# Turning keys and queries in 32x32 blocks on VectorE and by short store runs, in place of TensorE turns

## The chip, the cores and the metric

The kernel runs on one core of a Trainium2 chip. The metric is the device time of one execution in microseconds. Before the change it is 1336.66 us, the median of 3 runs (1335.41 to 1338.84).

The engines are named as in the profile: PE is TensorE's matmul queue and PEld its weight loads, DVE is VectorE, ACT is ScalarE, POOL is GpSimd, SP is SyncE, which only issues DMAs here. ACT and POOL issue DMAs too.

## The reference

One layer of a diffusion block over 512 tokens of width 2048, with 256 context tokens, all in float32. Cut to what matters:

```python
h  = rmsnorm(x) modulated by the conditioning vector      # 512 x 2048
hc = rmsnorm(ctx) modulated likewise                      # 256 x 2048
p  = h @ w_in                                             # q, k, v, z_a, u_b, z_b, g_a, g_b
kc, vc = rmsnorm per head of (hc @ w_in[:, K]), hc @ w_in[:, V]
q = rope(rmsnorm per head of q) * 128 ** -0.5             # 12 heads of 128
k = rope(rmsnorm per head of k)                           # 4 heads of 128
attn = softmax(q @ [k, kc].T) @ [v, vc]                   # 3 query heads per key head, 768 keys
y_a = (attn * silu(z_a)) @ w_proj_a
y_b = (fft2(u_b) * silu(z_b)) @ w_proj_b
x  = x + gate * ((sigmoid(g_a) * y_a + sigmoid(g_b) * y_b) @ w_out)
return rmsnorm(x) * final_g
```

The score product needs queries and keys with the head's 128 channels along the partitions. The projections leave them with the tokens along the partitions, so both must be turned somewhere between the projection and the scores.

## The kernel before

Matrix products are made in float32 accuracy from float32r halves: each operand is split into a high part (ACT, a copy, L162) and a low part (DVE, a subtraction, L163), and `mm3` issues three matmuls (L294 high by high, L295 high by low, L296 low by high). `split_from` is the helper for one split.

The projection after the first stage is made in groups of 1024 output columns, g = 0 to 7, of the kinds `KINDS`: three "qz" groups (queries of four heads and their z), two "gate", one "kv" (g = 5), two "gate". Each group computes its four quarters (two token halves by two column halves) from seven products (P1, Q5, P2, Q6, P7, Q3, Q4) of four weight pieces each. A piece of 512 KB is loaded by SP's queue (L198, L201) or added onto a running sum by an accumulating POOL DMA (L250), combined by DVE where needed (L239, L241), split by ACT and DVE, and then used by 12 matmuls. `get` splits pieces ahead of their use, up to as many as there are buffers for split pieces (3, or 5 for most of the time). A stop of ACT, DVE or the loads therefore reaches TensorE only once these ready pieces are used up.

After P2 the quarter (half 0, queries) is ready, after Q4 the quarter (half 1, queries); after P7 and Q3 those of z. `qz_done` and, for g = 5, `kv_done` take them:

- `rotated` (L827) squares each head on ACT for its norm (L836), multiplies by cosines and sines on DVE (L838, L840), adds the two (L843) and scales by the norm's root (L844). The result r lies in the buffer qr, the only one for this, and so the next rotated half can't begin to write before the stores of the one before have landed.
- Two stores per half, issued by ACT (L858 for queries and z, L868 for keys and values), write 128 tokens each to a DRAM buffer, one 512-byte run per token and head. `qz_d` has for each head and token partition the queries and z of its four token tiles.
- In the kv group the context's keys and values are made beside the tokens' (`Context`). `keys` normalizes the context keys in half of a buffer called cxe, which shares its place with a raw load buffer, and stores them (L926).

After the last query half, `context_norm` (L942) writes a diagonal into the first columns of qr, for the context's norms. After group 5, the space of qr is given to two more raw load buffers; loads into them on SP's queue wait for the key stores to land.

The program is written in the order of the loops, with a list `jobs` of deferred steps of which one is run per weight piece. A planner then sets the order on each engine's queue by its own costs and due times, so that steps of `rotated` lie scattered among the splits.

Attention runs 48 steps, one per head and tile of 128 queries. `scores` multiplies with all 768 keys into a pair of PSUM banks tagged "x", takes the maximum on DVE (L1117) and the exponentials on ACT (L1119); `turn` turns the probabilities on TensorE (L1135), `values` multiplies them by the values, and `filler` fills in products of the other branch. Around the change:

- `load_head` loads queries and z of a head from qz_d by a POOL DMA (L1003).
- `turn_queries` (L1014) turns a head's four query tiles on TensorE into a PSUM bank (L1016) that the products with the values also use, and splits them from there. This is done at the second step of the head before.
- `get_keys` (L1005) takes the raw keys of a key head from their load buffer, turns six tiles of 128 keys on TensorE into an "x" pair (L1009), and splits them from PSUM. The first key head is taken before the last product of the last group, the others at steps 10, 22 and 34.

Of the kernel before, what the change touches and what calls it, by code (L numbers as in the profile page):

```python
# [18 lines left out]
P = 128  # L19
# [88 lines left out]
def block_kernel(ctx, tc, xT, ctx_rows, ctx_toks, x, c_row, w_ss, w_gate, vecs, qkg, rope, dft_c, dft_s,  # L108
# [718 lines left out]
    def rotated(half, v, t2):  # L827

        v = v.rearrange("p t (h d) -> p t h d", h=4)
        r, t2 = new_q(), t2.rearrange("p t (h d) -> p t h d", h=4)  # L830
        ss = sums[:, 8 * half : 8 * half + 8]
        r5 = lambda w: w.rearrange("p h (a f j) -> p h a f j", a=2, f=2)
        for b in range(2):
            cosb, sinb = (turning[:, i, 2 * half + b, None, :].broadcast_to([P, 4, HD]) for i in range(2))
            for h in range(4):
                nc.scalar.activation(t2[:, b, h, :], v[:, b, h, :], ACT.Square,  # L836
                                     accum_out=ss[:, 4 * b + h : 4 * b + h + 1])
            nc.vector.tensor_tensor(r[:, b], v[:, b], cosb, op=ALU.mult)  # L838
# [5 lines left out]
        nc.vector.tensor_tensor(r, r, ss.rearrange("p (t h) -> p t h", t=2)[:, :, :, None].broadcast_to([P, 2, 4, HD]),  # L844
                                op=ALU.mult)
        return r

    def qz_done(half, c, v, t):

        if c:  # L850
            e = pair("x" if half else "y")
            nc.scalar.activation(e, v, ACT.Tanh, scale=0.5)
            nc.vector.scalar_tensor_tensor(v, e, 1.0, v, op0=ALU.add, op1=ALU.mult)
            r = v.rearrange("p t (h d) -> p t h d", h=4)
        else:
            r = rotated(half, v, pair("y"))
        for b in range(2):
            nc.scalar.dma_start(qz_d[4 * group.g : 4 * group.g + 4, :, c, 2 * half + b, :].rearrange("h p d -> p h d"),  # L858
                                r[:, b])

    by_group = lambda v: v.rearrange("g p d -> p g d")

    def kv_done(half, c, v, t):


        r = v.rearrange("p t (g d) -> p t g d", g=4) if c else rotated(half, v, pair("y", 1) if half else pair("x"))
        for b in range(2):
            nc.scalar.dma_start(by_group((v_d if c else k_d)[:, :, 2 * half + b, :]), r[:, b])  # L868

    class Context:  # L870

# [45 lines left out]
        def keys(self, b, v):  # L917
# [8 lines left out]
            nc.scalar.dma_start(by_group(k_d[:, :, 4 + b, :]), k4)  # L926


    cparts = qr[:, :1792].rearrange("p (f j c) -> p f j c", f=7, j=2)
# [69 lines left out]
    qz, qs, kv = {}, {}, {}  # L999

    def load_head(h):
        qz[h] = take((2, 4, HD))
        nc.gpsimd.dma_start(qz[h], qz_d[h])  # L1003

    def get_keys(g):  # L1005
        raw = get(("K", g))
        tk = flat(pair("x"))
        for t in range(KT):
            nc.tensor.transpose(tk[:, t * P : (t + 1) * P], raw[:, t * P : (t + 1) * P], ident)  # L1009
        keys = tiles(g)  # L1010
        split_from(tk[:, :NKEY], *(w[:, :NKEY] for w in keys))
        kv[g] = tuple(keys) + get(("V", g))

    def turn_queries(h, tq):  # L1014
        for t in range(4):
            nc.tensor.transpose(tq[:, t * P : (t + 1) * P], qz[h][:, 0, t, :], ident)  # L1016
        qs[h] = take((2, T), F32R)
        split_from(tq, qs[h][:, 0, :], qs[h][:, 1, :])

    load_rotations(qkg[:, 0:2, :])  # L1020
    for g, kind in enumerate(KINDS):
# [13 lines left out]
        for name in ONE_GROUP:  # L1035
# [20 lines left out]
            elif (g, name) == (LAST, "Q4"):  # L1056
                hl_pools[:] = [p for p in hl_pools if not isinstance(p, int)]
                get_keys(0)
                jobs.append(lambda: turn_queries(0, pair("y")[:, 0, :]))
            group.run(name)  # L1060
    gvs.close()
    evs.close()
# [60 lines left out]
    def divide(i):  # L1123

        h, t = divmod(i, 4)
        z = qz[h][:, 1, t, :]
# [15 lines left out]
    def values(half):  # L1142
# [4 lines left out]
        for k in range(KT):  # L1147
            mm3(av[:, :256], vh[:, k, :], vl[:, k, :], pth[:, k, :], ptl[:, k, :], k == 0, k == KT - 1)
        for t in range(2):
            nc.tensor.transpose(av[:, 256 + t * P : 256 + (t + 1) * P], qz[h][:, 1, 2 * second + t, :], ident)  # L1150
        if second:
            give(qz.pop(h))
            if h % GQ == GQ - 1:
# [25 lines left out]
    for i in range(NSTEP + 3):  # L1179
# [18 lines left out]
            turn(i - 1)  # L1198
            divide(i - 1)
        if t == 1 and h + 1 < NH:  # L1200
            turn_queries(h + 1, b1())
        if want > filled:
            fill(want - filled)
            filled = want
# [360 lines left out]
```

## Time and profile before

| what | value |
|---|---|
| median of 3 runs | 1336.66 us |
| span of the profiled execution | 1334.5 us |
| PE busy | 1299.7 us, 97% |
| DVE busy | 978.1 us, 73% |
| ACT busy | 653.8 us, 49% |
| POOL busy | 138.0 us, 10% |
| DMA, mean rate | 218 GB/s, 291.28 MB |
| q1 (loads and stores issued by SP) | 37.2% of 16 engines |
| q0 (issued by POOL) | 28.7% |
| q10 (issued by ACT) | 5.1%, 22464 packets, 22.81 MB |
| TensorE's granted clock, mean | 0.998 |

The execution's own time outside the span is not shown, so the span is set beside the median of the runs. The three qz groups lie from about 170 to 400 us, with their last steps to 420, the kv group from about 557 to 671, attention from about 815 to 1005. Busy time of PE is pipelined: a 512-column matmul is shown with 0.39 us but the next one starts 0.23 us later, so starts tell more than durations. A number in brackets behind a row of the timeline is the engine's idle time just before it, with what ended it. A wait is given with its total, its count and its longest. In a row of a DMA queue stand packets, MB and the share of the time of 16 engines; in a row of DMA issues the KB of each and the median time from issue to landing in us.

### The profile page before, as it was taken

To read this page: it belongs to the slowest core of one execution; us is meant where nothing else is said; L and a number is where in the kernel's file an instruction comes from. 1 tells how busy PE (TensorE), PEld (TensorE's weight loads), DVE (VectorE), ACT (ScalarE), POOL (GpSimd) and SP (SyncE) were. 2 spreads that over 40 slices of the span, in tenths; PEclk is the share of its full clock that TensorE was granted. 3 is DMA by queue.
4 is the path that set the end of the run, shared out by engine and by line. 5 is a ranking of instruction groups with operands and counts; after the bars stand their busy time and mean duration, and the time that the engine had idled before them with its cause. 6 is when DMAs were issued, how large, how long until landed. Compare 5 with 4: busy or idle time off the path is not lost. (4 is left out here: it accounts for less than half of the span.)

```text
span 1334.5 us, 17496 instructions
## 1 busy us (share of the span) xinstructions
PE 1299.7 (97%) x6594; PEld 1061.6 (80%) x6594; DVE 978.1 (73%) x1289; ACT 653.8 (49%) x1018; POOL 138.0 (10%) x186
## 2 busy tenths in 40 slices
PE   7999999999999999999999999999999999999996
PEld 3566888888888887888888888888888888878884
DVE  4655989877778777646477766777776789687677
ACT  5322655555555545444254555656665233464534
POOL 1110011110302011011021110000000100110210
PEclk9999999999999999999999999999999999999999
DMA  9996677887897989767679886112113998778973
GB/s 382 408 377 243 228 188 203 226 228 224 197 311 191 323 246 267 256 159 181 190 196 307 218 230 219 41 60 79 48 48 114 342 348 303 186 157 242 229 208 126
DMA packets 96085, 291.28 MB, mean 218 GB/s; under 512 B 8960, under 2 KB 32000, under 8 KB 91648
## 3 DMA queue, kind: packets, MB, share of 16 engines
q1 hardware_dynamic: 51600, 172.95, 37.2%
q0 software_dynamic: 21936, 94.39, 28.7%
q10 hardware_dynamic: 22464, 22.81, 5.1%
q8 instruction: 52, 0.85, 0.2%
q14 instruction: 33, 0.27, 0.1%
HBM read 263.37 MB, written 26.75 MB: 217 GB/s over the span
## 5 line engine op out<-in xcount | busy, mean ns | idle before, releaser
L162 ACT ACTIVATE whi<-wr 128x1024 fp32r<-128x1024 f32 (+1 forms) x129 | 135.4, 1052 | 193.5 <-PE y L296 87.0
L294 PE MATMUL y<-whi,s 128*128 128x512 f32 x544 | 214.8, 395 | 1.1 <-ACT s L761 1.1
L295 PE MATMUL x<-wlo,s 128*128 128x512 f32 x548 | 213.6, 390 | 1.8 <-DVE wlo L163 1.8
L295 PE MATMUL y<-wlo,s 128*128 128x512 f32 x544 | 212.5, 391 | 2.0 <-DVE wlo L163 2.0
L294 PE MATMUL x<-whi,s 128*128 128x512 f32 x548 | 214.1, 391 | 0.2 <-ACT s L758 0.2
L296 PE MATMUL x<-whi,s 128*128 128x512 f32 x548 | 213.3, 389 | 0.0
L296 PE MATMUL y<-whi,s 128*128 128x512 f32 x544 | 211.9, 390 | 0.0
L163 DVE TENSOR_TENSOR wlo<-wr,whi 128x1024 fp32r<-128x1024 f32 (+1 forms) x129 | 155.8, 1211 | 60.1 <-ACT whi L162 59.9
L162 ACT ACTIVATE whi<-R 128x1024 fp32r<-128x1024 f32 x115 | 121.4, 1059 | 127.6 <-PE x L296 62.1
L163 DVE TENSOR_TENSOR wlo<-R,whi 128x1024 fp32r<-128x1024 f32 x115 | 139.7, 1220 | 51.2 <-ACT whi L162 51.2
L294 PEld LDWEIGHTS y<-whi,s 128*128 128x128 f32 x544 | 102.1, 188 | 24.8 <-DVE s L1159 2.3
L295 PEld LDWEIGHTS x<-wlo,s 128*128 128x128 f32 x548 | 102.9, 188 | 23.6 <-DVE wlo L163 2.6
L294 PEld LDWEIGHTS x<-whi,s 128*128 128x128 f32 x548 | 102.9, 188 | 21.9 <-ACT s L758 0.5
L296 PEld LDWEIGHTS x<-whi,s 128*128 128x128 f32 x548 | 102.9, 188 | 21.4
L295 PEld LDWEIGHTS y<-wlo,s 128*128 128x128 f32 x544 | 102.2, 188 | 21.8 <-DVE wlo L163 2.9
L296 PEld LDWEIGHTS y<-whi,s 128*128 128x128 f32 x544 | 102.1, 188 | 21.4
L294 PE MATMUL x<-s,s 128*128 128x512 f32 (+1 forms) x274 | 104.5, 381 | 4.2 <-ACT s L1119 3.1
L295 PE MATMUL x<-s,s 128*128 128x512 f32 (+1 forms) x284 | 106.5, 375 | 0.0
L296 PE MATMUL x<-s,s 128*128 128x512 f32 (+1 forms) x284 | 106.1, 374 | 0.0
L250 POOL DMA_DIRECT2D R<-in_w_g x64 | 55.4, 866 | 424.9 <-DVE wlo L163 313.9
L162 ACT ACTIVATE s<-wr 128x512 fp32r<-128x512 f32 (+2 forms) x94 | 61.7, 674 | 62.5 <-PE y L296 17.5
L163 DVE TENSOR_TENSOR s<-wr,s 128x512 fp32r<-128x512 f32 (+2 forms) x94 | 67.4, 742 | 24.4 <-ACT s L162 23.6
(275 smaller groups left out, 2257.2 us busy)
## 6 DMA issues: line engine op xcount, KB each, us to landing
wr<-in_w_g SPq DMA_DIRECT2D x128, 512.0 KB, 4.9
R<-in_w_g POOLq DMA_DIRECT2D x64, 512.0 KB, 7.1
wa<-in_w_ss POOLq DMA_DIRECT2D x28, 1024.0 KB, 8.9
R<-in_w_g SPq DMA_DIRECT2D x32, 512.0 KB, 5.1
wr<-in_w_pab SPq DMA_DIRECT2D x32, 512.0 KB, 5.1
wr<-in_w_gate SPq DMA_DIRECT2D x32, 512.0 KB, 5.7
wr<-in_w_o SPq DMA_DIRECT2D x24, 512.0 KB, 5.4
R<-in_w_o POOLq DMA_DIRECT2D x24, 512.0 KB, 6.5
```

The source lines that it names most:

```text
L162: nc.scalar.activation(hi, src, ACT.Copy)
L163: return nc.vector.tensor_tensor(lo, src, hi.bitcast(F32), op=ALU.subtract)
L250: nc.gpsimd.dma_start(chain[e.pc], e.nxt, accum_op=ALU.add)
L294: nc.tensor.matmul(o, ah, bh, start=start, stop=False, skip_group_check=cont)
L295: nc.tensor.matmul(o, ah, bl, start=False, stop=False, skip_group_check=cont)
L296: nc.tensor.matmul(o, al, bh, start=False, stop=stop, skip_group_check=cont)
```

## The change

Queries and keys are turned where they are made. `rotated` adds and scales in the PSUM pair t2, and `nc.vector.transpose` then writes r with each block of 32 tokens by 32 channels turned within its place. The stores put the blocks where they belong: for each group of 32 partitions (which now are channels) one DMA, and in it, for each of 32 partitions, 4 heads and 4 blocks of channels, one run of 32 tokens, which is 128 bytes. k_d and qz_d now hold each head as channels by tokens. Context keys go the same way. The stores of z and of values stay as they are.

On the loading side, a head's queries come with channels along the partitions, and only the split is left (`split_queries`). Keys are no longer a raw load that is turned; they are a stream piece that is split like a weight piece, into the tiles that `get_keys` used to fill, and so may be split ahead of `get_keys` by the look-ahead of `get`.

```diff
-    k_d = dsc.tile([NKV, P, KT, HD], F32, name="k_d")
+    k_d = dsc.tile([NKV, HD, NKEY], F32, name="k_d")
-    qz_d = dsc.tile([NH, P, 2, 4, HD], F32, name="qz_d")
+    qz_d = dsc.tile([NH, P, 2, T], F32, name="qz_d")
...
     def stream_keys(g):
-        stream(("K", g), flat(k_d[g]), NKEY, KT, "raw")
+        stream(("K", g), k_d[g], NKEY, 1, dst=lambda: tiles(g))
...
         root_of(ss)
-        nc.vector.tensor_tensor(r, r, t2, op=ALU.add)
-        nc.vector.tensor_tensor(r, r, ss.rearrange("p (t h) -> p t h", t=2)[:, :, :, None].broadcast_to([P, 2, 4, HD]),
+        nc.vector.tensor_tensor(t2, r, t2, op=ALU.add)
+        nc.vector.tensor_tensor(t2, t2, ss.rearrange("p (t h) -> p t h", t=2)[:, :, :, None].broadcast_to([P, 2, 4, HD]),
                                 op=ALU.mult)
+        nc.vector.transpose(r.rearrange("p t h d -> p (t h d)"), t2.rearrange("p t h d -> p (t h d)"))
         return r
+
+    def store_turned(dst, v, t):
+
+        v = v.rearrange("p h (c j) -> p h c j", j=32)
+        for a in range(4):
+            to = dst[:, :, t * P + 32 * a : t * P + 32 * a + 32].rearrange("h (c i) j -> i h c j", i=32)
+            nc.scalar.dma_start(to, v[32 * a : 32 * a + 32])
...
         for b in range(2):
-            nc.scalar.dma_start(qz_d[4 * group.g : 4 * group.g + 4, :, c, 2 * half + b, :].rearrange("h p d -> p h d"),
-                                r[:, b])
+            t, to = 2 * half + b, qz_d[4 * group.g : 4 * group.g + 4, :, c]
+            if c:
+                nc.scalar.dma_start(to[:, :, t * P : t * P + P].rearrange("h p d -> p h d"), r[:, b])
+            else:
+                store_turned(to, r[:, b], t)
...
         for b in range(2):
-            nc.scalar.dma_start(by_group((v_d if c else k_d)[:, :, 2 * half + b, :]), r[:, b])
+            if c:
+                nc.scalar.dma_start(by_group(v_d[:, :, 2 * half + b, :]), r[:, b])
+            else:
+                store_turned(k_d, r[:, b], 2 * half + b)
...
-            k4 = self.V.rearrange("p (h d) -> p h d", h=4)
-            nc.vector.tensor_tensor(k4, k4, ss[:, :, None].broadcast_to([P, 4, HD]), op=ALU.mult)
-            nc.scalar.dma_start(by_group(k_d[:, :, 4 + b, :]), k4)
+            by_head = lambda w: w.rearrange("p (h d) -> p h d", h=4)
+            nc.vector.tensor_tensor(by_head(v), by_head(self.V), ss[:, :, None].broadcast_to([P, 4, HD]), op=ALU.mult)
+            nc.vector.transpose(self.V, v)
+            store_turned(k_d, by_head(self.V), 4 + b)
...
     def get_keys(g):
-        raw = get(("K", g))
-        tk = flat(pair("x"))
-        for t in range(KT):
-            nc.tensor.transpose(tk[:, t * P : (t + 1) * P], raw[:, t * P : (t + 1) * P], ident)
-        keys = tiles(g)
-        split_from(tk[:, :NKEY], *(w[:, :NKEY] for w in keys))
-        kv[g] = tuple(keys) + get(("V", g))
-
-    def turn_queries(h, tq):
-        for t in range(4):
-            nc.tensor.transpose(tq[:, t * P : (t + 1) * P], qz[h][:, 0, t, :], ident)
+        keys = get(("K", g))
+        kv[g] = tuple(w[:, 0, :] for w in keys) + get(("V", g))
+
+    def split_queries(h):
         qs[h] = take((2, T), F32R)
-        split_from(tq, qs[h][:, 0, :], qs[h][:, 1, :])
+        split_from(qz[h][:, 0, :], qs[h][:, 0, :], qs[h][:, 1, :])
```

The calls follow: `split_queries(h + 1)` stands where `turn_queries(h + 1, b1())` stood, `load_head` takes a (2, T) tile, and z is indexed by columns in `divide` and `values`.

More of the change, by code (lines that the diff above doesn't have):

```diff
@@ L1001, in load_head @@
     def load_head(h):
-        qz[h] = take((2, 4, HD))
+        qz[h] = take((2, T))
         nc.gpsimd.dma_start(qz[h], qz_d[h])
     def get_keys(g):
-        raw = get(("K", g))
-        tk = flat(pair("x"))
-        for t in range(KT):
-            nc.tensor.transpose(tk[:, t * P : (t + 1) * P], raw[:, t * P : (t + 1) * P], ident)
-        keys = tiles(g)
-        split_from(tk[:, :NKEY], *(w[:, :NKEY] for w in keys))
-        kv[g] = tuple(keys) + get(("V", g))
-    def turn_queries(h, tq):
-        for t in range(4):
-            nc.tensor.transpose(tq[:, t * P : (t + 1) * P], qz[h][:, 0, t, :], ident)
+        keys = get(("K", g))
+        kv[g] = tuple(w[:, 0, :] for w in keys) + get(("V", g))
+    def split_queries(h):
         qs[h] = take((2, T), F32R)
-        split_from(tq, qs[h][:, 0, :], qs[h][:, 1, :])
+        split_from(qz[h][:, 0, :], qs[h][:, 0, :], qs[h][:, 1, :])
     load_rotations(qkg[:, 0:2, :])
@@ L1058, in block_kernel @@
                 get_keys(0)
-                jobs.append(lambda: turn_queries(0, pair("y")[:, 0, :]))
+                jobs.append(lambda: split_queries(0))
             group.run(name)
@@ L1125, in divide @@
         h, t = divmod(i, 4)
-        z = qz[h][:, 1, t, :]
+        z = qz[h][:, 1, t * P : t * P + P]
         r = stats[:, 4 * (i % 4) + 2 : 4 * (i % 4) + 3]
@@ L1149, in values @@
         for t in range(2):
-            nc.tensor.transpose(av[:, 256 + t * P : 256 + (t + 1) * P], qz[h][:, 1, 2 * second + t, :], ident)
+            nc.tensor.transpose(av[:, 256 + t * P : 256 + (t + 1) * P], qz[h][:, 1, (2 * second + t) * P : (2 * second + t + 1) * P], ident)
         if second:
@@ L1200, in block_kernel @@
         if t == 1 and h + 1 < NH:
-            turn_queries(h + 1, b1())
+            split_queries(h + 1)
         if want > filled:
```

## The prediction

> **What bounds the kernel now.** I read the page first, then the busy time by stage, the waits, then the lines that the change touches.
>
> ```profile
> PE 1299.7 (97%) x6594; PEld 1061.6 (80%) x6594; DVE 978.1 (73%) x1289; ACT 653.8 (49%) x1018; POOL 138.0 (10%) x186
> ...
> 160.00:245.00 85.00, 84.98 (x423) 72.07 (x422) 77.64 (x94) 45.15 (x66) 9.77 (x12) 1.00 0.74 200
> 245.00:330.00 85.00, 85.00 (x377) 70.38 (x376) 69.84 (x81) 45.11 (x87) 13.06 (x13) 1.00 0.81 218
> 330.00:420.00 90.00, 90.00 (x399) 74.53 (x398) 70.17 (x84) 51.66 (x99) 19.19 (x19) 1.00 0.88 240
> 590.00:690.00 100.00, 100.00 (x443) 82.75 (x442) 68.17 (x75) 42.26 (x88) 14.80 (x16) 1.00 0.64 175
> 690.00:760.00 70.00, 69.64 (x308) 57.34 (x307) 48.33 (x53) 35.17 (x43) 6.04 (x7) 1.00 0.91 273
> 820.00:1005.00 185.00, 179.31 (x1178) 157.40 (x1177) 133.30 (x230) 114.76 (x201) 4.22 (x8) 1.00 0.20 64
> ```
>
> The columns of a stage are its window and length in us, busy time (and count) of PE, PEld, DVE, ACT and POOL, the granted clock, the DMA share and GB/s. TensorE has no idle time to speak of in the three query groups (160 to 420), in most of the key group and the next one (590 to 690) and after it, at a full clock; only attention (820 to 1005) shows 5.7 us of it. So what leaves TensorE's queue shortens the kernel one for one, and what stops VectorE or the loads costs only what TensorE's stock of ready weight pieces doesn't cover. DVE is busy for 78% to 91% of the query groups and DMA for 74% to 88%: these must take the added work.
>
> **Off TensorE: the turns.**
>
> ```profile
> L1016 PE MATMUL y<-ident,s x48: 271/272/330, 816.1 to 998.3; 128*128 128x128 f32 x48
> ...
> L1009 PE MATMUL x<-ident,wr x24: 270/272/327, 812.7 to 962.9; 128*128 128x128 f32 x24
> ...
> 812.50 0.39 PE L296 MATMUL y<-s,s 128*128 128x512 f32 x1
> 812.73 0.82 PE L1009 MATMUL x<-ident,wr 128*128 128x128 f32 x6
> 813.30 0.47 PE L294 MATMUL x<-whi,s 128*128 128x512 f32 x1
> 813.61 0.39 PE L295 MATMUL x<-wlo,s 128*128 128x512 f32 x1
> ...
> 815.90 0.40 PE L296 MATMUL x<-whi,s 128*128 128x512 f32 x1
> 816.14 0.60 PE L1016 MATMUL y<-ident,s 128*128 128x128 f32 x4
> 816.49 0.48 PE L294 MATMUL x<-whi,s 128*128 128x512 f32 x1
> 816.81 0.39 PE L295 MATMUL x<-wlo,s 128*128 128x512 f32 x1
> ```
>
> The 272 ns of one turn overlap their neighbours, so I price them by starts. From the ordinary matmul before a head's four turns to the second one after them there are 816.81 - 815.90 = 0.91 us, where two ordinary steps (812.50 to 812.73) take 0.46: a head costs 0.45 us, and 12 heads 5.4. A group's six key turns cost 813.61 - 812.50 - 0.46 = 0.65 us, and four groups 2.6. Together 8.0 us. One head and one key group lie in the stage before attention, where TensorE is never idle (1.1 us); the other 6.9 lie in attention.
>
> [...]
>
> **The wait in attention.**
>
> ```profile
> PE x L294 <- ACT s L1119: 3.1, 5, 1.1
> ...
>   ACT s L1095: 0.5, 2
> ...
>   ACT s L1119: 1.4, 2
> ```
>
> Of TensorE's 5.7 idle us there, 3.1 wait for ScalarE's exponentials to free a score bank. With fewer turns TensorE comes to those banks sooner. Against that, the turns no longer wait for banks themselves, 0.5 us ahead of the queries' (L1016) and 1.4 ahead of the keys' (L1009) on its queues, the last two rows. The splits of keys and queries stay as long as they are, and read SBUF in place of PSUM. I set the two against each other and take nothing (bounds: 1 us gained, or 3 lost, a doubling of the first row). Keys are now split with the piece look-ahead, ahead of need, and leave the raw buffers sooner; I cost that at nothing, as DMA is busy for 20% of this stage and ACT for 62%; without that cover it is one split, about 1 us, per group.
>
> **On VectorE: ten turns.**
>
> ```profile
> L844 DVE TENSOR_TENSOR qr<-qr,small 128x1024 f32<-128x1024 f32 x8 | 9.8, 1219 | 0.3
> ...
> L838 DVE TENSOR_TENSOR qr<-ev,qr 128x512 f32<-128x512 f32 x8 | 5.1, 682 | 0.0
> ```
>
> No 32x32 turn is in this trace. One pass over 128x1024 takes 1.22 us and over 128x512 0.68, so eight turns of queries and keys and two of context keys are 8 x 1.22 + 2 x 0.68 = 11.1 us if they go at the rate of a pass (which I take), and twice that if at half the rate. The sum and the product that now write PSUM I leave at their price. Each query group gets 2.4 us where DVE is idle for 7 to 20 us. Behind each turn stand the splits of later pieces. How long VectorE may stop is measured here:
>
> ```profile
> 701.60 1.23 DVE L241 TENSOR_TENSOR wr<-R,wr 128x1024 f32<-128x1024 f32 x1 [6.98 <-DMA wr<-in_w_g]
> ...
> 704.02 0.50 PE L295 MATMUL y<-wlo,s 128*128 128x512 f32 x1 [0.36 <-DVE wlo L163]
> ```
>
> VectorE stood 6.98 us for a load, and TensorE lost 0.36: the stock covers some 6.6 us. A turn of 1.2 us is within that. I take 0.5 us in all, for the first query group, where DVE has the least room (bounds 0 and 3).
>
> **On ScalarE's queue and the DMA engines: 18 stores become 72.**
>
> ```profile
> L858 ACTq DMA_DIRECT2D qz_d<-qr x12: 366/452/677, 218.5 to 417.3; - x12
> ...
> L926 ACTq DMA_DIRECT2D k_d<-cxe x2: 366/372/377, 611.4 to 677.6; - x2
> ...
> q10 hardware_dynamic: 2112, 1.05, 22.8%
> ...
> q0 software_dynamic: 48, 0.01, 5.8%
> ```
>
> A half's two stores become eight, so ScalarE issues 6 x 0.45 = 2.7 us longer (a context half: 3 x 0.37 = 1.1), and the splits behind it wait that long. ACT is busy for little over half of these stages; covered by the stock, cost nothing, else at most 2.7 us for each of the eight halves.
>
> The runs shrink from 512 to 128 bytes, so each store of 256 KB goes from 512 to 2048 of them, 128 for each DMA engine. The q10 row is the window 384:400, with four stores in 512-byte runs only: 0.228 x 16 us x 16 / 2112 = 28 ns a run. The q0 row is the window 1139:1149.6, whose one q0 transfer is gs<-gcol, 2048 elements of 4 bytes: 0.058 x 10.6 x 16 = 9.8 us, 4.8 ns each. A 128-byte run lies between; by bytes it comes to 10 ns, which I take: 1.3 us of all engines per store for 0.9 before, nothing beside a group of 85 us. At 28 ns it would be 3.6, so 2.7 more, 11 us in each query group.
>
> **What waits for the stores.** All rotated halves share the buffer qr, so the next writer waits until they have landed.
>
> ```profile
> 416.93 1.08 ACTq L858 DMA_DIRECT2D qz_d<-qr  x2
> 420.90 0.28 DVE L942 TENSOR_SCALAR qr<-ident,small 128x128 f32<-128x128 f32 x1 [2.87 <-DMA qz_d<-qr]
> ...
> 340.33 1.05 ACTq L858 DMA_DIRECT2D qz_d<-qr  x2
> qz_d<-qr ACTq DMA_DIRECT2D x2, 256.0 KB, 9.4
> 360.11 0.68 DVE L838 TENSOR_TENSOR qr<-x,qr 128x512 f32<-128x512 f32 x1
> ...
> DMA to landing us min/median/max: 2.4/4.6/12.0
> ...
> SPq L198 <- DMA k_d<-qr: 11.9, 1, 11.9
> SPq L198 <- DMA k_d<-cxe: 9.2, 1, 9.2
> k_d<-qr ACTq DMA_DIRECT2D x2, 256.0 KB, 17.3
> ...
> 705.03 1.14 SPq L198 DMA_DIRECT2D wr<-in_w_g  x2
> ```
>
> The tight place is L942 after the last query half. It already holds VectorE 2.87 us, with weight splits queued behind it. The stores now start 1.2 us later, the last is issued some 2.7 us after its old time, and if it lands as fast as today VectorE stands 2.9 + 3.9 = 6.8 us: about 0.2 us past the cover. I take 1 us, as that place may have less stock than the one measured; if the planner sets L942 later in VectorE's queue, it is 0, and rival 1 has the other end. At L838 there are 20 us from issue (340.33) to the next writer; these two stores took 9.4 us (window 339.5:353), and no qz_d store over 12: nothing. The last key stores (17.3 us to landing, window 686:706) hold SP's queue, with all weight loads behind, for 11.9 us, and a context store for 9.2; both get longer by 3 to 5 us. The first loads behind the long wait went out at 705.03, after TensorE's pause at 704.02, which a load ahead of that wait had caused; so the wait itself has cover, and I cost both together at 1 us (bounds: 0, and the 5 of rival 1).
>
> **Sum.** -8.0 + 0 (attention) + 0.5 (VectorE) + 1.0 (L942) + 1.0 (SP) = -5.5 us. The profiled span of 1334.5 becomes 1329.0. The profile gives nothing around the span; the median of the runs is 2.2 us above it, and I keep that: 1336.7 - 5.5 = 1331.2 us. A difference under 0.3% (4 us) can't be told from none here.
>
> **Rivals.**
> 1. *The small runs land late, and VectorE and SP stand for them (slower).* The nearest row for busy engines is the last key store: 17.3 us for two stores, 64 runs per engine, 0.27 us a run, as if each run waited its turn behind a weight packet; the 416.93 pair took 3.9 us, 0.06 us a run. If turns go by the run and not by the byte, 256 runs take 16 us at L942 in place of 3.9: VectorE stands 2.9 + 1.2 + 12 = 16, TensorE loses 9. After 340 they take 256 x 0.15 (two stores at 9.4 us, 64 runs) = 38 us against 20, so VectorE stands some 19; the loads dry up meanwhile and free the engines, so I take half, 9.5, less the cover of 6.6: 3. The last key store lands 10 to 15 us later: 5, an estimate. 9 + 3 + 5 - 8.0 + 0.5 = +9.5: 1346. It decides from about 0.1 us a run. For it: DMA shares of 0.88 and 0.91. Against it: 28 ns a run with four stores in 16 us.
> 2. *A run of 128 bytes costs an engine what one of 512 does.* Then the query groups' DMA share rises by 11/85: 0.88 becomes 1.0. If a quarter of the 11 us can't be hidden in the three query groups and in the key group, 4 x 2.7 = 11 us are lost beside the 2.5 of the sum: -8.0 + 2.5 + 11 = +5.5: 1342. For it: 28 ns for only 512 bytes; against it, 4.8 ns for 4 bytes. [...]
> 3. *Attention is set by the exponentials, not by TensorE.* Then half of the 6.9 us turns into waits for L1119, and with the stalls above 3 us are gained or less: 1334 to 1337. For it: 3.1 us of such waits stand there already; against it: TensorE is busy for 97% of the stage and ACT for 62%.
>
> **How the numbers follow.** Forecast 0.50, its own range 1328 to 1332.6 by the bounds (all 8.0 gained and 1 us of bank waits too: 1328; stalls of 4 us in place of 2.5: 1332.7). Rival 3: 0.26, no change to be measured. Rival 1: 0.14 and rival 2: 0.10, both slower. So faster 0.50, same 0.26, slower 0.24. The range 1328 to 1345 leaves out the far part of rival 1 and something below.
>
> **What would show it.** Right: L1009 and L1016 gone, TensorE's busy time in 820 to 1005 down by some 6.9 us with idle time near 5.7; ten new DVE turns near 1.2 and 0.7 us; q10's share per run near 10 ns; L942 waiting for qz_d by 6 to 8 us without a pause of TensorE. Wrong: TensorE idle in 400 to 440 or 690 to 730 for over 2 us with wlo as releaser, landings of qz_d over 18 us, DVE waits at L838 for qz_d, SP held for k_d beyond 20 us (rival 1); DMA share at 0.95 and over in 245 to 420 (rival 2); waits for L1119 of 6 us and more (rival 3).

## The result and the profile after

The changed kernel takes 1349.01 us (median, 1346.34 to 1350.22) against 1337.75 us for the kernel before (1335.41 to 1340.24): a ratio of 1.0082, 95% interval 1.0063 to 1.0101, so 0.8% or 11 us slower. The profiled executions have spans of 1347.5 and 1334.5 us, 13.0 us apart.

The page's row of busy times for the changed kernel, and the answer by windows, with the columns that the prediction explains:

```profile
PE 1298.7 (96%) x6522; PEld 1056.8 (78%) x6522; DVE 985.9 (73%) x1299; ACT 651.3 (48%) x1018; POOL 136.9 (10%) x186
```

```profile
160.00:245.00 85.00, 84.98 (x431) 72.47 (x431) 77.47 (x94) 45.16 (x69) 9.78 (x12) 1.00 0.74 194
245.00:330.00 85.00, 85.00 (x377) 70.41 (x376) 70.12 (x82) 44.48 (x88) 11.55 (x12) 1.00 0.82 211
330.00:420.00 90.00, 89.15 (x392) 72.93 (x391) 72.90 (x88) 51.03 (x99) 17.67 (x17) 1.00 0.85 229
505.00:590.00 85.00, 79.56 (x341) 65.04 (x340) 55.06 (x64) 36.79 (x46) 6.06 (x8) 0.96 0.85 238
590.00:690.00 100.00, 95.81 (x408) 78.03 (x408) 55.77 (x58) 34.23 (x59) 7.25 (x9) 0.97 0.63 165
690.00:760.00 70.00, 60.65 (x259) 49.19 (x258) 47.35 (x56) 32.72 (x60) 11.48 (x12) 0.93 0.81 219
820.00:1005.00 185.00, 184.05 (x1140) 160.04 (x1139) 140.90 (x230) 121.02 (x202) 5.86 (x11) 1.00 0.31 99
```

The same window that the prediction doesn't show, of the kernel before:

```profile
505.00:590.00 85.00, 82.88 (x365) 67.99 (x364) 54.17 (x56) 40.39 (x50) 6.82 (x8) 1.00 0.82 232
```

Attention (820 to 1005) has become better: TensorE idles for 0.95 us where it idled for 5.7. The three query groups (160 to 420) are as full as they were, but for 0.85 us in the last. The loss lies in 505 to 760: 3.3, 4.2 and 9.0 us less of TensorE's time in the three windows, and in each the granted clock is 0.93 to 0.97, where it was 1.00 before. The timeline of TensorE there, in the changed kernel (start, length, instruction; in brackets the idle time ahead of it and what ended it):

```profile
532.23 0.80 PE L295 MATMUL x<-wlo,s 128*128 128x512 f32 x1 [5.44 <-DVE wlo L163]
...
632.41 1.22 PE L294 MATMUL y<-whi,s 128*128 128x512 f32 x2 [4.16 <-ACT whi L162]
...
638.10 0.63 PE L296 MATMUL y<-whi,s 128*128 128x512 f32 x1
638.53 0.48 PE L295 MATMUL y<-wlo,s 128*128 128x512 f32 x1
638.84 0.39 PE L296 MATMUL y<-whi,s 128*128 128x512 f32 x1
639.07 0.40 PE L294 MATMUL y<-whi,s 128*128 128x512 f32 x1
...
719.76 0.79 PE L294 MATMUL x<-whi,s 128*128 128x512 f32 x1 [8.89 <-ACT whi L162]
```

Three pauses, 18.5 us together. Two of them end with ScalarE's split `whi` (L162). After each of them the matmuls go at about half the pace for a while: the 13 from 632.41 to 638.53 take 6.1 us, 0.47 each, at a granted clock of 0.50 in that stretch, and then they follow each other at 0.23, so some 3 us more are lost there, and about 2.5 in the same way after 719.76. The half pace lasted 6.1 us after 4.16 us of idle time, 4.4 us after 8.89 (granted clock 0.51) and 4.0 us after 5.44, at 532.23 (0.50).

What ScalarE did before those two splits, in the timeline of ScalarE (rows with ACTq are the issues of DMAs on its queue):

```profile
622.68 1.59 ACTq L854 DMA_DIRECT2D k_d<-cxe  x3
626.42 4.22 ACTq L854 DMA_DIRECT2D k_d<-qr  x8
630.68 0.52 ACTq L854 DMA_DIRECT2D k_d<-cxe  x1
631.30 1.06 ACT L162 ACTIVATE whi<-R 128x1024 fp32r<-128x1024 f32 x1 [11.26 <-DMA k_d<-qr]
...
706.13 12.47 ACTq L854 DMA_DIRECT2D k_d<-qr  x8
718.65 2.00 ACT L162 ACTIVATE whi<-wr 128x1024 fp32r<-128x1024 f32 x2 [13.39 <-DMA k_d<-qr]
```

It did nothing else: it stood 11.26 and 13.39 us, with the next split behind the eight stores of a key half on its queue (L854 is the `dma_start` in `store_turned`). The first stretch, from 620.0 on, holds more than those eight: ScalarE waits for VectorE's turns until 622.68 and again until 626.42, and it issues four stores of the context's keys (`cxe`). In the second half the eight issues alone take 12.47 us where eight of 0.45 would take 3.6. All issues of that line (fewest, median and most ns of one), and the landing:

```profile
L854 ACTq DMA_DIRECT2D qz_d<-qr x48: 309/520/5867, 222.2 to 434.2; - x48
...
L854 ACTq DMA_DIRECT2D k_d<-qr x16: 309/520/6782, 626.4 to 718.1; - x16
...
DMA to landing us min/median/max: 1.8/4.2/11.6
```

The median issue costs 0.52 us, but some take 5.9 and 6.8. So an issue can block, and the split behind it on ScalarE's queue waits with it (13.39 us at 718.65). In the set of 706.13 the first three went out in 0.7 us or less each, and the fourth took 6.78.

### The profile page after: what moved, and what is told of

The parts are those of the page before. It is cut to its first block, busy times and chain, and to the rows that moved or that the text cites. A ratio compares the mean times of both kernels' runs of the same rounds, so it can differ in the third digit from the quotient of the medians.

```text
span 1347.5 us, 17425 instructions
## 1 busy us (share of the span) xinstructions
PE 1298.7 (96%) x6522; PEld 1056.8 (78%) x6522; DVE 985.9 (73%) x1299; ACT 651.3 (48%) x1018; POOL 136.9 (10%) x186
## 5 line engine op out<-in xcount | busy, mean ns | idle before, releaser
L162 ACT ACTIVATE whi<-wr 128x1024 fp32r<-128x1024 f32 (+1 forms) x129 | 135.3, 1052 | 223.5 <-PE y L296 75.1
L162 ACT ACTIVATE whi<-R 128x1024 fp32r<-128x1024 f32 x115 | 120.7, 1057 | 119.7 <-PE y L296 46.6
L296 PEld LDWEIGHTS x<-whi,s 128*128 128x128 f32 x548 | 103.8, 189 | 21.6
L162 ACT ACTIVATE s<-wr 128x512 fp32r<-128x512 f32 (+2 forms) x98 | 65.2, 681 | 75.5 <-PE y L296 23.5
L163 DVE TENSOR_TENSOR s<-wr,s 128x512 fp32r<-128x512 f32 (+2 forms) x98 | 71.2, 749 | 27.2 <-ACT s L162 26.3
```

The source lines that it names most:

```text
L162: nc.scalar.activation(hi, src, ACT.Copy)
L163: return nc.vector.tensor_tensor(lo, src, hi.bitcast(F32), op=ALU.subtract)
L296: nc.tensor.matmul(o, al, bh, start=False, stop=stop, skip_group_check=cont)
```

## The experiments

In the expectations, theory A is, where nothing else is said beside it, that ScalarE's queue is held by the issues of the turned stores, so that the splits behind them come late; the rivals have other letters, explained where they stand. Ratios are to the kernel before, on the same chip.

| kernel | turned by VectorE | turned stores: issues, runs, queue | median us | ratio, 95% interval |
|---|---|---|---|---|
| the change | queries, keys | 72, 128 B, ScalarE | 1349.01 | 1.0082 (1.0063 to 1.0101) |
| e1 | queries | 48, 128 B, ScalarE | 1333.04 | 0.9949 (0.9931 to 0.9967) |
| e2 | queries, keys | 18, 512 B, ScalarE | 1332.38 | 0.9949 (0.9934 to 0.9965) |
| e3 | queries, keys | 72, 512 B, ScalarE | 1334.83 | 0.9975 (0.9958 to 0.9991) |
| e4 | queries, keys | 18, 128 B, ScalarE | 1333.44 | 0.9958 (0.9941 to 0.9976) |
| e5 | keys | 24, 128 B, ScalarE | 1356.71 | 1.0129 (1.0108 to 1.0150) |
| e6 | queries, keys | 16 of 72 on GpSimd | 1331.34 | 0.9948 (0.9928 to 0.9967) |
| e7 | queries, keys | 72, 128 B, GpSimd | 1327.87 | 0.9923 (0.9902 to 0.9944) |
| e8 | queries | 12, 512 B, ScalarE | 1326.17 | 0.9905 (0.9886 to 0.9924) |
| e9 | queries, keys | 12, 512 B, ScalarE; 24, 128 B, GpSimd | 1326.05 | 0.9901 (0.9884 to 0.9919) |
| e10 | none | the 18 of before, GpSimd | 1343.42 | 1.0036 (1.0024 to 1.0048) |
| e11 | queries, three times | as e8 | 1329.56 | 0.9935 (0.9923 to 0.9947) |
| e12 | queries, keys | as the change; three pairs | 1383.52 | 1.0330 (1.0311 to 1.0350) |
| e13 | queries, keys | as e7; three pairs | 1342.13 | 1.0013 (0.9997 to 1.0028) |
| e14 | queries, keys | 72, 128 B, SyncE | 1328.32 | 0.9918 (0.9899 to 0.9938) |
| e15 | queries, keys | as the change; first key half later | 1342.36 | 1.0028 (1.0010 to 1.0046) |
| e16 | queries, keys | as the change; both key halves later | 1338.39 | 1.0000 (0.9987 to 1.0013) |

### Which part: queries alone, keys alone

e1 leaves the keys as before; e5 leaves the queries as before.

```diff
 e1, in kv_done (rotated leaves out the turn, get_keys is that of before):
-        r = ... rotated(half, v, pair("y", 1) if half else pair("x"))
+        r = ... rotated(half, v, pair("y", 1) if half else pair("x"), False)
-                store_turned(k_d, r[:, b], 2 * half + b)
+            nc.scalar.dma_start(by_group(k_d[:, :, 2 * half + b, :]), r[:, b])
 e5: the same in qz_done, with turn_queries as before
```

> Keys are stored in 512-byte runs and turned by TensorE as before; queries go as in the change. Theory A (the store issues hold ScalarE's queue, and the key group with three split buffers can't cover it): TensorE's pauses of 4.2 and 8.9 us around the key group go, and with them some 6 us of slow clock; the queries' 5.4 us and part of attention's idle time stay gained: 1328 to 1332. Theory B (VectorE's turns and the PSUM detour make the rotated halves late everywhere): the query groups would show pauses of the same kind, 1338 or more.

> Only keys are turned by VectorE and stored in 128-byte runs (24 store issues); queries as before, turned by TensorE. Theory A (ScalarE's in-order queue is held by the key stores' issues, and the key group has only three split buffers): issues of k_d take up to 5 to 8 us again, ScalarE's splits wait 10 to 15 us for them, TensorE pauses of 4 to 9 us near 630 and 718 with ScalarE's whi as releaser; ratio 1.008 to 1.014 (-2.6 us for 24 turns, +19 for the two pauses). Rival B (it is the two parts together: 72 short-run stores and later query stores push the key group): no pause over 3 us there, ratio 0.996 to 1.001.

Queries alone are 5.7 us faster than before, keys alone 18.7 us slower (medians): the loss is the keys'. e5's timeline of TensorE and its issues have the two pauses of the changed kernel again, and its window of attention has nearly the idle time of before, 4.85 us for 5.7:

```profile
627.02 1.22 PE L294 MATMUL y<-whi,s 128*128 128x512 f32 x2 [4.17 <-ACT whi L162]
714.45 0.80 PE L294 MATMUL x<-whi,s 128*128 128x512 f32 x1 [8.83 <-ACT whi L162]
```

```profile
L859 ACTq DMA_DIRECT2D k_d<-qr x16: 309/517/6915, 621.0 to 712.8; - x16
```

```profile
820.00:1005.00 185.00, 180.15 (x1119) 156.12 (x1119) 133.91 (x217) 113.74 (x190) 5.85 (x11) 1.00 0.29 93
```

So the keys' part makes the two pauses without any help from the queries' (e5's rival falls), and the gain in attention belongs to the queries. In e1 ScalarE is held for query stores too, up to 12.3 us at a time, and TensorE loses under 2 us to that in the query groups; one pause of 3.87 us stands at 534.72.

### What holds ScalarE: the number of issues or the size of the runs

e2 to e4 keep all of VectorE's turns. e2 writes a turned tile as it stands in SBUF, one store in runs of 512 bytes, and its 128-byte runs are read by the loads; e3 cuts that store in four by partitions; e4 writes 128-byte runs, but with one issue per tile in place of four. In all three the loads are made with the layout, too.

```diff
     def store_turned(dst, v, t):
-        v = v.rearrange("p h (c j) -> p h c j", j=32)
-        for a in range(4):
-            to = dst[:, :, t * P + 32 * a : t * P + 32 * a + 32].rearrange("h (c i) j -> i h c j", i=32)
-            nc.scalar.dma_start(to, v[32 * a : 32 * a + 32])
 e2: +        nc.scalar.dma_start(dst[:, t].rearrange("h a i c j -> (a i) h (c j)"), v)
 e3: +        for a in range(4):
     +            nc.scalar.dma_start(dst[:, t, a].rearrange("h i c j -> i h (c j)"), v[32 * a : 32 * a + 32])
 e4: +        nc.scalar.dma_start(dst[:, :, t].rearrange("h c a i j -> (a i) h c j"),
     +                            v.rearrange("p h (c j) -> p h c j", j=32))
```

> All turns stay on VectorE, but the turned blocks are stored as they lie, one store of 512-byte runs for 128 tokens (18 issues as before), and the 128-byte runs are read by the loads in attention, four per head and per key head. Theory A: ScalarE is held no longer than before, no pause of TensorE over 1 us in the key group, 1324 to 1330. Theory B: the pauses of 4 and 9 us stay, since the turns stay: 1340 to 1349. If the short loads come late in attention, pauses there with a load as releaser, some us more.

> As the run with stores as they lie, but each store cut into four of 32 partitions: 72 issues, 512-byte runs. If the number of issues holds ScalarE (0.5 us each, more when the engines are busy): eight issues still take 4 to 12 us, pauses in the key group stay, 1336 to 1346. If it is the number of runs that must find room (512 in one issue of the change, 128 here): eight issues take under 4 us even when busy, 1325 to 1331.

> As the run with stores as they lie, but with a layout in which each of the 18 stores writes 2048 runs of 128 bytes in one issue. If the number of issues holds ScalarE: two issues take about 1 us, time as with stores as they lie, 1324 to 1330. If the number of runs does: the two issues of a half take 4 to 12 us together, pauses of 4 and 9 us at the key group, 1336 to 1348.

The issues of e2, of e3 and of e4:

```profile
L857 ACTq DMA_DIRECT2D q_d<-qr x12: 366/453/1081, 221.3 to 422.7; - x12
...
L857 ACTq DMA_DIRECT2D k_d<-qr x4: 366/452/636, 617.2 to 689.1; - x4
```

```profile
L858 ACTq DMA_DIRECT2D q_d<-qr x48: 309/458/593, 225.0 to 432.6; - x48
L858 ACTq DMA_DIRECT2D k_d<-qr x16: 309/455/511, 623.5 to 714.3; - x16
```

```profile
L857 ACTq DMA_DIRECT2D q_d<-qr x12: 366/684/4953, 221.5 to 422.1; - x12
...
L857 ACTq DMA_DIRECT2D k_d<-qr x4: 366/1214/7251, 619.1 to 691.0; - x4
```

In 512-byte runs no issue of queries or key halves takes over 1.1 us, be they 18 or 72 (one of e3's context stores takes 2.17); in 128-byte runs some take 5 and 7 us, be they 18 or 72. So it is the run size that makes these issues block; e4's longest one ends in a hold of 8.77 us and a pause of TensorE of 6.47 us, at 699.45. But ScalarE can be held without any long issue. The second key half of e3, in ScalarE's timeline:

```profile
702.53 12.06 ACTq L858 DMA_DIRECT2D k_d<-qr  x8
714.63 1.67 ACT L163 ACTIVATE s<-wr 128x512 fp32r<-128x512 f32 x3 [11.52 <-DMA k_d<-qr]
```

Its eight issues take 0.31 to 0.51 us each, and yet 12.06 in all, as there are waits between them. The seventh goes out as soon as the first has landed (at 709.4) and the eighth as soon as the second has (at 714.3). So the number of issues holds ScalarE, too, and "under 4 us even when busy" was wrong; but three splits that stand behind the stores in the change stand ahead of them here, and TensorE loses only 1.25 us to the hold.

By the clock the three are close, with intervals that overlap, and none is within the times expected of it: all lie between the lower and the upper forecasts, as e1 does by 1 us. e2 is no clean base for them, as it has a pause of its own, 5.37 us at 716.65, after VectorE has stood 9.98 us for a weight load. The change, with both the many issues and the short runs, is nearly 18 us above e2 by the ratios; its stores also stand elsewhere on the queue (see "Place in the queue" below). All three are faster than before with every turn on VectorE, so that VectorE's work is the cause is refuted.

### Moving the stores off ScalarE

```diff
-            nc.scalar.dma_start(to, v[32 * a : 32 * a + 32])
 e6: nc.gpsimd for the two key halves, nc.scalar for the rest
 e7: nc.gpsimd for all         e14: nc.sync for all
 e10: the kernel before, its 12 + 4 + 2 stores of rotated queries and keys by nc.gpsimd
```

> The changed kernel, but the 16 turned stores of the two key halves are issued by GpSimd instead of ScalarE; same runs of 128 bytes, same bytes, same turns. Theory A: the pauses with ScalarE's whi as releaser near 632 and 720 go, no ScalarE wait for k_d over 3 us; 12 to 19 us less than the changed kernel: ratio 0.994 to 1.000. Rival B (late landing or busy DMA engines: whoever issues, the stores end late and hold SP's weight loads or the splits): pauses of over 3 us remain there, ratio 1.004 and over.

> All 72 turned stores issued by GpSimd. Theory A: also the waits of ScalarE for qz_d in the query groups (5 to 12 us) go; ratio 0.992 to 0.998, at or below the kernel with only the key stores moved. Rival C (GpSimd's own issue of 512 short runs is slow, and the shared buffer qr is freed late): VectorE waits at L838 or L942 for qz_d by over 7 us, ratio above that of the kernel with only the key stores moved by 0.003 or more.

> The changed kernel with its 72 turned stores issued by SyncE, whose queue carries the weight loads. Theory A (an issue blocks the queue that it stands on, and what is queued behind it is late): ScalarE no longer waits for the stores; issues of up to 5 to 8 us and the waits for VectorE's turn stand on SP's queue instead, weight loads come 10 to 15 us later, and the splits wait for raw weights: ratio between the GpSimd one and 1.01, so 0.995 to 1.012, with pauses after waits for wr. Rival H (it is only ScalarE's queue that can't take it; SP's loads are early enough): 0.992 to 0.994.

> The kernel before, with its 18 stores of rotated queries and keys issued by GpSimd instead of ScalarE; all turns by TensorE as before. Control. Theory A (512-byte runs do not hold ScalarE): within 0.003 of 1. Rival E (moving stores off ScalarE is itself the gain of the moved kernels): ratio 0.994 or less.

With nothing changed but the queue of 16 issues, e6 is 18 us faster than the change by the ratios (0.0134 of 1338), and its two windows are full:

```profile
590.00:690.00 100.00, 100.00 (x441) 82.32 (x440) 64.66 (x72) 39.17 (x83) 16.67 (x21) 1.00 0.63 166
690.00:760.00 70.00, 69.45 (x306) 56.93 (x305) 52.82 (x56) 36.31 (x45) 12.59 (x17) 1.00 0.91 278
```

e7 is 3 us lower still, but the two intervals overlap. Its issues on GpSimd, and those of e14's key halves on SyncE:

```profile
L854 POOL DMA_DIRECT2D qz_d<-qr x48: 648/651/756, 221.3 to 428.3; - x48
L854 POOL DMA_DIRECT2D k_d<-qr x16: 648/651/702, 618.9 to 699.5; - x16
```

```profile
L854 SPq DMA_DIRECT2D k_d<-qr x16: 302/603/5042, 622.4 to 705.8; - x16
```

None of e7's issues on GpSimd takes over 0.76 us; e14's on SyncE can block, up to 5.04 us, and yet e14 is as fast as e7: the expectation that the weight loads behind them would come too late was wrong, rival H was right. No pause of TensorE in e14's groups is over 1.8 us, so SyncE's loads had a lead that ScalarE's splits have not. The control e10 shows that leaving ScalarE is no gain in itself: it makes the kernel before 0.4% slower, a little more than either theory allowed (a pause of 3.57 us at 708.16 is new). In the change eight starts took 12.47 us on ScalarE. Moving the starts is worth some 21 us (e7 against the change, by the ratios), though not all of that is their time.

### Place in the queue, or issues that block

The moves take away the stores' place in ScalarE's order, too. Before the change the planner had put three splits between the last squares of the first key half and its stores; in the changed kernel the stores come right behind the squares. So ScalarE waits for VectorE's turn (L846, done at 626.4) with splits behind it, and then issues for 4.2 us, none of which blocks. e15 emits the first half's eight stores later, which puts two splits ahead of them; e16 does it in both halves, with four splits ahead of the second half's stores.

```diff
-                store_turned(k_d, r[:, b], 2 * half + b)
+                later.append((r[:, b], 2 * half + b))
+        if not c:
+            todo_k = [later.pop(0) for _ in range(2)]
+            jobs.extend([lambda: None] * 3 + [lambda: [store_turned(k_d, v, t) for v, t in todo_k]])
 e16: (3, 6)[half] in place of 3
```

> The changed kernel; the first key half's eight stores are put two splits later in ScalarE's order, by ScalarE still, in 128-byte runs. Theory P (their place ahead of those splits made the first pause): no pause over 1 us near 630, the second (8.9 us near 718) as it was: some 8 us less than the changed kernel, ratio 1.000 to 1.004. Theory I (issue time and short runs, wherever they stand): the first pause stays at 3 us or more, ratio 1.006 to 1.010.

> As before, and the second key half's eight stores stand four splits later. Theory P: both pauses under 2 us, ratio 0.994 to 0.998, near the kernels with stores on other queues. Theory I (issues that block hold ScalarE 12 us wherever they stand, more than the stock of three pairs covers): ScalarE held 10 us or more there again and a pause of 3 us or more after it, ratio 0.999 to 1.004.

ScalarE around the first key half in e15, and TensorE's pause after the second:

```profile
624.34 3.72 ACTq L854 DMA_DIRECT2D k_d<-cxe  x4
628.17 1.06 ACT L162 ACTIVATE whi<-R 128x1024 fp32r<-128x1024 f32 x1 [6.47 <-DVE qr L846]
628.28 0.99 ACTq L854 DMA_DIRECT2D k_d<-qr  x2
629.13 1.05 ACT L162 ACTIVATE whi<-wr 128x1024 fp32r<-128x1024 f32 x1
629.31 3.36 ACTq L854 DMA_DIRECT2D k_d<-qr  x6
632.71 1.06 ACT L162 ACTIVATE whi<-wr 128x1024 fp32r<-128x1024 f32 x1 [2.53 <-DMA k_d<-qr]
```

```profile
713.97 0.79 PE L294 MATMUL x<-whi,s 128*128 128x512 f32 x1 [8.82 <-ACT whi L162]
```

(Rows of issues overlap with the splits ahead of them, which the engine works off meanwhile.) The hold of 11.26 us has become two, 6.47 for VectorE's turns and the context's stores and 2.53 behind the key stores, with two splits between; TensorE has no pause there, and some 7 us are back (0.0054 by the ratios), with the same eight issues in the same 128-byte runs. The second pause stands as it was. So the first pause was one of place, as theory P had it. In e16 the second half is this:

```profile
701.50 12.32 ACTq L854 DMA_DIRECT2D k_d<-qr  x5
713.94 1.15 ACT L162 ACTIVATE s<-wr 128x512 fp32r<-128x512 f32 x2 [15.49 <-DMA k_d<-qr]
```

```profile
714.63 0.80 PE L294 MATMUL x<-s,s 128*128 128x512 f32 x1 [5.30 <-ACT s L162]
```

Three of the eight issues go out early, and the last five still take 12.32 us. The splits ahead shorten TensorE's pause from 8.89 to 5.30, no more: what is left of the second pause is made by issues that block, as theory I had it, though not against a stock of three pairs, as the next section shows.

### Why the query groups got away with it

In the query groups ScalarE is held for 5 to 13 us six times, and TensorE hardly notices. There five pairs of split buffers (whi, wlo) hold ready weights, in the key group three. The first pause stands there: when ScalarE comes to the stores, at 620.0, TensorE has ready pieces until 628.25, three of 2.7 us. The second pause stands in the group after it, where the kernel has five pairs again. But when ScalarE comes to the stores there, at 705.3, only two pieces are ready (TensorE stops at 710.87); shortly before, ScalarE itself had waited 3.95 and 1.17 us for VectorE's sums R. e12 and e13 give the query groups three pairs, with the stores on ScalarE and on GpSimd:

```diff
             if (g, name) == (0, "Q5"):
-                hl_pools += range(MORE_HL)
```

> The changed kernel (stores on ScalarE), with three pairs of split buffers in place of five in query groups and up to the key group. Theory A (the stock decides): pauses of TensorE of 3 to 9 us in the query groups too, with ScalarE's whi as releaser, six holds there; 15 to 40 us over the changed kernel (1.008): ratio 1.02 to 1.04, and at least 12 us more than its control with the stores on GpSimd gains over the changed kernel. Rival F (it is something else in the key group, the stock of three being enough): within 5 us of the changed kernel, 1.005 to 1.012, no pause over 2 us in 245 to 420.

> Control: all turned stores on GpSimd, with three pairs of split buffers in the query groups. Theory A: nothing holds ScalarE for long, so within 6 us of five pairs (0.9923): 0.990 to 0.997. Rival G (three pairs are too few for the query groups whatever the stores do): 5 us and more over that, 0.998 and up, with pauses at the ends of query halves that VectorE or ScalarE ends.

TensorE's longest pause in 245 to 420, in e12 (a second one there is 4.80 us long) and in e13:

```profile
286.80 0.79 PE L294 MATMUL x<-whi,s 128*128 128x512 f32 x1 [5.37 <-ACT whi L162]
```

```profile
354.59 0.79 PE L295 MATMUL y<-wlo,s 128*128 128x512 f32 x1 [3.36 <-DVE wlo L163]
```

Fewer pairs cost 12 us by themselves (e13 against e7 by the ratios, so theory A's expectation for e13 was too low and rival G's right), but with the stores on ScalarE they cost 33 us (e12 against the change), and pauses that ScalarE ends appear where there were none. In the query groups the size of the stock decides whether a hold is seen. The reverse, five pairs in the key group, was not run.

### The price of VectorE's turns, and the fastest version

e8 turns queries alone on VectorE and stores them as e2 does; e9 adds keys turned on VectorE, stored in 128-byte runs by GpSimd. e11 is e8 with each turn made three times.

```diff
 e11: +nc.vector.transpose(t2, r); nc.vector.transpose(r, t2)    (after the turn of t2 into r)
```

> Queries turned by VectorE but stored whole in runs of 512 bytes (12 issues), their 128-byte runs read by the loads in attention; keys as before. Theory A: issues of q_d at most 1.1 us, no ScalarE wait for them over 3 us, -5.4 us of turns and up to 4 of attention's waits, +0.5 for VectorE: ratio 0.992 to 0.996, at or below queries alone with short runs (0.9949). Rival D (the gain is bounded by VectorE's turns, not by the issues): same as queries alone, 0.9949 within 0.001, with pauses of TensorE that VectorE's wlo ends in the query groups.

> Queries turned by VectorE, stored in 512-byte runs by ScalarE; keys turned by VectorE too, stored in 128-byte runs by GpSimd (24 issues). If the two repairs add (theory A): the 24 turns of keys off TensorE too, 2.6 us, so ratio 0.987 to 0.991 against 0.9905 with keys as before. Rival (the key group has no room for the VectorE turns, or for the later landing of key stores): pauses of over 2 us near 630 or 715, ratio 0.992 to 0.997.

> The kernel with blocked query stores and keys as before, with each of the six turns of VectorE done three times (there, back, there: the output is the same): 12 more passes of 1.24 us, 14.9 us of VectorE. Theory A (VectorE's turns are covered by the stock of split weights): ratio 0.990 to 0.993, at most 2 us more than with one turn. Rival D (turns are on the path): 5 us and more, ratio 0.994 or over, with pauses in the query groups that VectorE ends.

e8 is 12 us under the kernel before, below the ratios expected of it, and no other is faster by more than its interval. e9 equals it: the 24 turns of keys that it takes off TensorE, 2.6 us by the prediction's rows, don't show. In e11 twelve more turns (VectorE is busy for 996.7 us in place of 983.7) cost about 3.5 us (medians 1329.56 and 1326.17, spans 1327.5 and 1323.8; 4.0 by the ratios, whose intervals just meet), between the two theories. Its one longer pause is in the first query group (in e8 it is 1.16 us):

```profile
232.54 0.54 PE L301 MATMUL y<-s,s 128*128 128x512 f32 x1 [3.41 <-DVE s L164]
```

## Why the prediction was wrong

The forecast was 1331.2 us; 1349.01 was measured.

**The step that failed** is ScalarE's: "6 x 0.45 = 2.7 us longer", "covered by the stock, cost nothing, else at most 2.7 us for each of the eight halves". The length of the hold was wrong: 11 and 13 us in place of 3.6. Two things were left out of it. An issue was given its median price of before; it can block, and with 128-byte runs it did, for up to 6.8 us in the change and 7.3 in e4 (e2 to e4, e16). The stores were taken to stay where they were on ScalarE's queue; the planner put those of the first key half ahead of three splits, where ScalarE waits for a VectorE chain that had become longer by its turn (e15), and those of the second ahead of two. The cover was nearer: 6.6 us were read from a stall of VectorE, and the holds show 7.1 (11.26 us and a pause of 4.16), 4.5 (13.39 and 8.89), and none lost at 6.47. But it was read as one number for all places, from a place with five pairs, and it goes with the pieces that are ready: three in the key group, two at the second hold. Each long pause then cost 2 to 3 us more at half pace, which the sum had not at all. The bound of 2.7 us for each half, 21.6 in all, was named but went into neither the range nor a rival.

**The 72 turns off TensorE, -8.0:** right in kind; the size can't be read apart. Their lines are gone. e7 and e8, which have no long hold, have spans 10.7 us under the kernel before.

**Attention, 0 with bounds -1 to +3:** wrong, and outside its bounds. Idle time fell from 5.7 to 0.95 us, and of the 3.1 us of waits for exponentials this is left in the changed kernel (the line is L1127 now):

```profile
PE x L294 <- ACT s L1127: 0.9, 3, 0.3
```

Rival 3, the only one of the cases to be about attention, is refuted. e5 ties the gain to the queries' turns; which resource they had held there, banks or the splits' place, was not tested.

**VectorE, 0.5:** the turn was priced rightly, and hides less than was thought:

```profile
L846 DVE STREAM_TRANSPOSE qr<-y 128x1024 f32<-128x1024 f32 x7 | 8.7, 1239 | 0.0
```

1.24 us for 1.22 predicted. By e11's rate, 3.5 us for 13.0, the ten turns would cost 3 us in place of 0.5, an estimate; the place was the predicted one, the first query group.

**The DMA engines:** 10 ns were taken for a 128-byte run, 28 by rival 2. A window with eight query stores and nothing else on that queue, 255 to 285, has

```profile
q10 hardware_dynamic: 4224, 0.52, 11.5%
```

0.115 x 30 us x 16 / 4224 = 13.1 ns. So a short run is dearer by the byte (0.10 ns against 0.055), cheaper by the run (13.1 ns against 28), and the shares of the three query groups stayed at 0.74, 0.82 and 0.85. Rival 2 is refuted as a bound of the kernel.

**VectorE and SyncE standing for the landing (L942, SP; rival 1):** no pause follows from either, so nothing is seen of the 1.0 us that the sum had for each. At the place of the old L942 VectorE doesn't wait for qz_d at all. SyncE is held 15.2 us for key stores in place of 11.9. Rival 1 had the sign, the size (1346) and the short runs right, and the wrong engine: it isn't VectorE that stands until they have landed, it is ScalarE that stands until they are taken.

**The sum again, with what was measured:** -8.0 for the turns (as predicted), -4.8 in attention and 0.5 to 3 for VectorE take 1334.5 to between 1322.2 and 1324.7 us, and e7 has a span of 1323.8. The change has 1347.5, 23.7 more: against e7's windows (82.59, 100.00 and 69.55 us busy) 3.0, 4.2 and 8.9 us of pauses, and the rest is mostly the half pace after them.

**What stays open.** The pause at 532 was not varied by itself. VectorE's timeline of the changed kernel shows what stands ahead of it:

```profile
530.35 0.69 DVE L816 SCALAR_TENSOR_TENSOR qr<-qr 128x512 f32<-128x512 f32 x1 [8.21 <-DMA qr<-in_qkg]
```

VectorE waits there for a load into qr, with the low part of a split (`wlo`) behind it on its queue. ScalarE issues this load at 519.1 in place of 511.6, and it lands after 11.1 us in place of 3.2; in the kernel before VectorE doesn't wait for it. The pause is 3.9 to 5.4 us long, and this wait 6.6 to 8.2, in all five kernels with five pairs in which ScalarE issues the query stores as 48 short-run pieces (the change, e1, e6, e15, e16). In the others the pauses near there are 2.2 us at most, and none has the wait. Why the load goes out later and lands more slowly is open. Nor was it tested what an issue waits for when it blocks.

## What to carry to other kernels

Count a DMA issue on a compute engine as an instruction that can block (on ScalarE here for 6.78 us, in 128-byte runs): if a store is cut into shorter runs, ask what stands behind it on the issuing engine's queue, not only when it lands. Put such stores on a queue with slack (e7 and e14, ratios 0.9923 and 0.9918), or keep the long runs on the store and take the short ones on a load that has time (e2 and e8, 0.9949 and 0.9905). A stock of ready pieces is a number for each place, at most that of the buffers and less where the splits are late (three and two pieces at the two holds here), and a hold that exceeds it is paid in idle time (4.16 and 8.89 us here) and again in the slow clock after it (some 3 and 2.5 us).

## What the runs showed of the hardware

Issues of 64 KB in 512 runs of 128 bytes can block on ScalarE's queue: at 706 us, in a window with a DMA share of 0.81, the fourth of eight takes 6.78 us, while the eight at 626 (0.63) take 0.52 each at most. On SyncE the longest was 5.04, and on GpSimd all 72 took 0.65 to 0.76. With runs of 512 bytes none of queries or key halves took over 1.1 us, and one of the context's 2.17. Eight such issues of 0.51 us at most still held ScalarE for 11.52 us in e3, by waits between them, of which the last two ended when earlier ones landed.
